# RWKV heads that alternate on the array, and four edits at the end of a two-layer hybrid block

## The chip, the cores and the metric

One core of a Trainium2 chip runs the whole program. The metric is device microseconds of one execution, median of three runs. Five engines work side by side, each through its own queue and in its order: PE (TensorE, matrix products, with its weight loads PEld), DVE (VectorE), ACT (ScalarE), POOL (GpSimd) and SP (SyncE, which issues most DMAs). A matmul of fp32 operands shows as two records of PE in the trace, one of fp32r (the format of the split products) as one.

## The reference, cut to what matters

The block has 256 latent and 256 context tokens of width 1024 and two layers. The change lies in the second layer's RWKV-7 mixer, in its expert sum and in the last norm.

```
# RWKV-7, per head (8 heads of 64), forward and backward over the tokens
def step(s, inp):
    rt, wt, kt, vt, at, bt = inp
    sa = einsum('bhij,bhj->bhi', s, at)
    s = s * wt[:, :, None, :] + sa[..., None] * bt[:, :, None, :] + vt[..., None] * kt[:, :, None, :]
    return s, einsum('bhij,bhj->bhi', s, rt)

# layer 1: S5 and RWKV side by side, then the experts, each with its residual and norm
yl = concatenate([oc_l, od_l], axis=-1)
xl = layer_norm(DEEPNORM_ALPHA * xl + gt1 * (yl @ w_out), ln_g[layer, 0], ln_b[layer, 0])
hl = xl * (1.0 + sc2) + sh2
for e in range(N_EXPERTS):                      # top 2 of 8, gates 0 elsewhere
    out = out + gates[..., e:e + 1] * swiglu(h, wg[e], wu[e], wd[e])
xl = layer_norm(DEEPNORM_ALPHA * xl + gt2 * f, ln_g[layer, 1], ln_b[layer, 1])
```

## The kernel before

The program goes through layer 0 (gated recurrence and attention, dense SwiGLU), the second layer's input products, the stage of S5 and RWKV, the output product with its norm and routing, eight experts, and the last norm. A scheduler fixes the order of each engine's queue when the program is built. Within a queue nothing overtakes: an instruction that waits holds up all behind it.

RWKV's tokens are cut into chunks of 64. The recurrence runs over eight steps `i` in two directions `d` (`SEQ`); steps 0 to 3 are the context, 4 to 7 the latent tokens. Eight heads are held as four pairs `p` of two heads `h`; head h = 0 lies on partitions 0 to 63, h = 1 on 64 to 127. All these products are small, and each uses one part of the array: a product of 64 rows by 64 columns uses a quarter, one of 128 by 64 a half, one of 32 by 32 a sixteenth. Where the two heads follow each other in the code, the parts that they use differ in the columns, the rows or both.

A step (`rwkv_units`, L1834 to L1917) goes: `pq` (state times `lk`, the heads alternate already) -> ACT copies it to `uR` (L1885) -> `pz` (the inverse `uY` times `uR`: four products of head 0, four of head 1) -> copies into `vu`, head 0 by ACT, head 1 by DVE (L1892) -> `ph` (`zh` times `vu`, again head by head) -> DVE adds it to the decayed state `ulT` and writes the new state `uT` (L1907) -> `pq` of the next step. Beside the chain stand `pi`, the 32 by 32 products that complete the inverse for the next step (`unit_inverse`, L1808 to L1828, two rounds with a copy by `evac` between), `gram` and `ztr`, which prepare units two steps ahead (`unit_before`, L1757 to L1806), and the outputs `po` of the latent steps (`outputs`, L1848 to L1862), which run one step late. For each direction and head a `po` bank holds four results; each result is the sum of a product of 128 rows (`uz` times `vu`) and one of 64 rows (`uRr` times `uT`), written in turn. Four products fill 64 rows of the bank, and a copy by ACT or an addition by DVE (L1862) moves them into `rO`.

S5 is put among these steps by generators: `tp<-U,wb` on PE, four multiplications, a sum, a scan and eight `xs` on DVE (L1392 to L1406), then `tp<-ca,xs` on PE. `rwkv_finish` (from L1923) normalises `rO` by heads on DVE and POOL and passes it to the output product.

An expert's last part (`expert`, L2217 to L2237) multiplies the down product by `g`, splits it into `myh` (ACT, L2223) and `myl` (DVE, L2224), and puts the rows back to their tokens by two fp32r products with `back` each; DVE adds the result, weighted, to `x` (L2234). After the eighth expert `norm_out` (L2276 to L2302) does the last norm for two tiles of 128 tokens: statistics, `rstd` (a chain of tiny operations, L205 to L218), and then two operations of DVE per half of 512 columns (L2297, L2298); the first half of tile 0 goes through ACT (L2293) and POOL (L2294, L2295) instead. At the end every engine loads a count of tokens (L2265) and branches on it (L2266).

Of the kernel before, what the change touches and what calls it, by code (L numbers as in the profile page):

```python
# [8 lines left out]
F32 = mybir.dt.float32  # L9
F32R = mybir.dt.float32r  # L10
I32 = mybir.dt.int32
U32 = mybir.dt.uint32
AF = mybir.ActivationFunctionType
OP = mybir.AluOpType
# [151 lines left out]
class Build:  # L166
# [39 lines left out]
    def rstd(self, pool, var, n, eps, op=OP.add):  # L206
# [6 lines left out]
        V.tensor_scalar(y.bitcast(I32), s.bitcast(I32), -1.0, 1597463007.0, op0=OP.mult, op1=OP.add)  # L213
        for _ in range(3):
            V.tensor_mul(w, y, y)
            V.scalar_tensor_tensor(w, w, -0.5, v, op0=OP.mult, op1=OP.mult)
            V.scalar_tensor_tensor(y, w, 1.5, y, op0=OP.add, op1=OP.mult)
# [1539 lines left out]
    def unit_before(self, i, d, rp, lk, zh, zp=None):  # L1757
# [18 lines left out]
        if lat:  # L1776
# [6 lines left out]
            for h in range(2):  # L1783
                pg = p128(f"gram{d}{i}")
                for p in range(4):
                    self.mm(pg[:, p], X[h2(h), p, 0:128], X[h2(h), p, 128:256], True, True)
# [21 lines left out]
    def unit_inverse(self, rp, i, d):  # L1808
# [8 lines left out]
        pb = rp.tile([128, 4, 32], F32, name="uP", tag="uP", bufs=2)  # L1817
        for h in range(2):
            r, o = slice(h * 64 + 32, h * 64 + 64), slice(h * 64, h * 64 + 32)
            for p in range(4):  # L1820
                self.mm(pi[o, 0, p], W[r, p], Y[r, p, 32:64], True, True)
            self.evac(pb[o], pi[o, 0])
        for h in range(2):
            o = slice(h * 64, h * 64 + 32)
            for p in range(4):
                self.mm(pi[o, 1, p], W[o, p], pb[o, p], True, True)
            self.evac(Y[o, :, 32:64], pi[o, 1])
        return Y  # L1828

    def rwkv_units(self, ra, rp, done, inv, room):  # L1830
# [17 lines left out]
        def outputs(i, Ss, vus):  # L1848

            for d in range(2):  # L1850
                n, rows = self.PLACE[self.SEQ[d][i]]
                z, X, S, vu = before[i, d][1], before[i, d][3], Ss[d], vus[d]
                for h in range(2):
                    po = self.psum_mx(f"po{d}{i}")[:, :256].rearrange("p (a b) -> p a b", b=64)
                    for p in range(4):
                        self.mm(po[rows, p], z[:, p, h], vu[:, p, h], True, False)
                        self.mm(po[rows, p], X[h2(h), p], S[h2(h), h, p], False, True)
                    o = O[rows, n].rearrange("p (a h v) -> p a h v", a=4, h=2)[:, :, h]
                    if (d == 0) == (self.SEQ[d][i] < 6):
# [465 lines left out]
```

## Time and profile before

| what | value |
|---|---|
| median of 3 runs | 2151.57 us (2148.89 to 2158.67) |
| the profiled execution, its span | 2162.4 us, 2160.6 us |
| PE busy | 2019.5 us, 93% |
| DVE busy | 1624.6 us, 75% |
| ACT busy | 1048.2 us, 49% |
| POOL busy | 176.3 us, 8% |
| read from and written to HBM | 442.56 MB, 31.98 MB |

The span is the time from the first to the last instruction that the profiler saw. Busy time counts an engine's own work; PE's is modelled at the ends, and the records of pipelined products overlap, so two figures are used for a product: its busy time, and the time from the start of one row to the start of the next. PEclk is the clock that TensorE was granted, as a share of full speed (1.0 is 2.4 GHz, 0.5 is 1.2 GHz); over a stretch it is a mean.

### The profile page before, as it was taken

Reading aid. Unit: us, or ns where it says so; the run is one execution under the profiler, and the core shown is the slowest. Engines: PE = TensorE matmul, PEld = TensorE weight load, DVE = VectorE, ACT = ScalarE, POOL = GpSimd, SP = SyncE. Lnnn points to the kernel's source line nnn. Section 1 sums busy time; section 2 is a strip of 40 time slices with the busy share of each in tenths; the row PEclk is TensorE's granted clock in tenths of the full one; section 3 lists DMA queues with packets and bytes.
Section 4 is the critical chain, followed back from the end, with each engine's and each line's share of the span. In section 5 each row is a group of like instructions: output and inputs, shape, how many; then the busy total and the mean of one; then the engine's idle time right before and its main releaser. Section 6 shows DMA issues by size and latency. Waiting matters only on the chain. (4 is left out here: it accounts for less than half of the span.)

```text
span 2160.6 us, 31186 instructions
## 1 busy us (share of the span) xinstructions
PE 2019.5 (93%) x11518; PEld 1591.5 (74%) x11518; DVE 1624.6 (75%) x3051; ACT 1048.2 (49%) x1604; POOL 176.3 (8%) x222
## 2 busy tenths in 40 slices
PE   7999999999999997895799979999999999999994
PEld 4766777777888876583688857788887777777773
DVE  3566756798777687877554287898989888888886
ACT  3334434332333335651222236777767777677762
POOL 1000000001000011004441033000000000000000
PEclk9999999999999999896666578999999999999997
DMA  8434223347566563477762175999989899998890
GB/s 301 124 109 147 80 78 97 130 151 231 197 195 192 152 169 126 141 226 240 194 177 76 32 267 202 359 344 354 348 328 341 328 346 327 347 331 333 325 357 21
DMA packets 148756, 476.66 MB, mean 221 GB/s; under 512 B 54020, under 2 KB 72532, under 8 KB 113524
## 3 DMA queue, kind: packets, MB, share of 16 engines
q1 hardware_dynamic: 120610, 428.13, 56.4%
q0 software_dynamic: 9648, 34.93, 5.1%
q10 hardware_dynamic: 18338, 11.54, 1.9%
q8 instruction: 92, 1.51, 0.3%
q14 instruction: 68, 0.56, 0.1%
HBM read 442.56 MB, written 31.98 MB: 220 GB/s over the span
## 5 line engine op out<-in xcount | busy, mean ns | idle before, releaser
L201 DVE TENSOR_TENSOR mwl<-mraw,mwh 128x1024 fp32r<-128x1024 f32 x522 | 617.7, 1231 | 57.1 <-ACT mwh L197 52.6
L197 ACT CAST mwh<-mraw 128x1024 fp32r<-128x1024 f32 x528 | 520.3, 1051 | 56.1 <-PE mm L179 32.2
L179 PE MATMUL mm<-hh,wl 128*128 128x512 f32 (+1 forms) x744 | 284.7, 384 | 7.8 <-DVE wl L201 7.8
L179 PE MATMUL mm<-hl,wh 128*128 128x512 f32 (+1 forms) x744 | 286.4, 386 | 4.4 <-DVE hl L452 4.4
L179 PE MATMUL mm<-hh,wh 128*128 128x512 f32 (+1 forms) x744 | 285.9, 387 | 2.7 <-ACT hh L451 2.3
L197 ACT CAST wh<-wraw 128x1024 fp32r<-128x1024 f32 x119 | 124.8, 1050 | 318.3 <-PE mm L179 243.8
L201 DVE TENSOR_TENSOR wl<-wraw,wh 128x1024 fp32r<-128x1024 f32 x119 | 145.1, 1220 | 85.8 <-ACT wh L197 79.5
L179 PE MATMUL mm<-mwh,hgh 128*128 128x512 f32 (+1 forms) x768 | 196.0, 377 | 4.1 <-ACT mwh L197 4.0
L179 PE MATMUL mm<-mwl,hgh 128*128 128x512 f32 (+1 forms) x768 | 196.7, 378 | 2.4 <-DVE mwl L201 2.4
L179 PE MATMUL mm<-mwh,hgl 128*128 128x512 f32 (+1 forms) x768 | 195.7, 377 | 0.0
L179 PEld LDWEIGHTS mm<-hh,wl 128*128 128x128 f32 x744 | 142.9, 192 | 36.7 <-DVE wl L201 9.2
L179 PEld LDWEIGHTS mm<-hh,wh 128*128 128x128 f32 x744 | 141.6, 191 | 34.3 <-ACT wh L197 4.4
L179 PEld LDWEIGHTS mm<-hl,wh 128*128 128x128 f32 x744 | 142.7, 192 | 31.8 <-DVE hl L452 4.8
L179 PEld LDWEIGHTS mm<-mwh,hgh 128*128 128x128 f32 x768 | 136.7, 188 | 34.9 <-ACT mwh L197 5.8
L179 PEld LDWEIGHTS mm<-mwl,hgh 128*128 128x128 f32 x768 | 136.0, 189 | 35.1 <-DVE mwl L201 7.3
L179 PEld LDWEIGHTS mm<-mwh,hgl 128*128 128x128 f32 x768 | 136.6, 188 | 28.6
L179 PE MATMUL mx<-mwh,mah 128*128 128x512 f32 x352 | 103.4, 402 | 1.1 <-ACT mwh L197 1.1
L179 PE MATMUL mx<-mwh,mal 128*128 128x512 f32 x352 | 104.0, 401 | 0.0
L179 PE MATMUL mx<-mwl,mah 128*128 128x512 f32 x352 | 99.8, 399 | 0.0
L179 PEld LDWEIGHTS mx<-mwh,mah 128*128 128x128 f32 x352 | 64.2, 188 | 20.4 <-ACT mwh L197 7.4
L179 PEld LDWEIGHTS mx<-mwl,mah 128*128 128x128 f32 x352 | 65.3, 188 | 14.1
L179 PEld LDWEIGHTS mx<-mwh,mal 128*128 128x128 f32 x352 | 64.7, 188 | 13.4
(600 smaller groups left out, 3283.6 us busy)
## 6 DMA issues: line engine op xcount, KB each, us to landing
mraw<-in_moe_w_dram SPq DMA_DIRECT2D x264, 1024.0 KB, 6.0
adaw<-in_ada_w_dram SPq DMA_DIRECT2D x96, 512.0 KB, 4.9
wraw<-in_ev_w_in_dram SPq DMA_DIRECT2D x26, 512.0 KB, 3.7
wraw<-in_ffn_w_gate_dram SPq DMA_DIRECT2D x22, 512.0 KB, 4.4
wraw<-in_ffn_w_up_dram SPq DMA_DIRECT2D x22, 512.0 KB, 4.4
wraw<-in_ffn_w_down_dram SPq DMA_DIRECT2D x22, 512.0 KB, 4.1
wraw<-in_od_w_in_dram SPq DMA_DIRECT2D x19, 512.0 KB, 4.0
d5ca<-ca POOLq DMA_DIRECT2D x32, 144.0 KB, 4.0
```

The source lines that it names most:

```text
L179: self.nc.tensor.matmul(out, lhsT, rhs, start=start, stop=stop, skip_group_check=True)
L197: self.nc.scalar.copy(hi, raw)
L201: self.nc.vector.tensor_sub(lo, raw, hi.bitcast(F32))
```

## The change

It has five parts. In `gram` of the latent chunks, `pi`, `pz` and `ph` the loop over heads goes inside the loop over pairs, so that the products of the two heads alternate; the copies follow when both heads are done, and the latent `gram` uses its two banks at once. In `outputs` both directions write one bank per head, into different row groups; first come all products of 128 rows, then all of 64 rows, with the directions in turn, and one copy or addition of 128 partitions replaces two of 64. The last expert's `back` and `my` stay fp32 and are multiplied without a split. The last norm is done by DVE alone, `rstd` of a single column has two operations fewer, and the output leaves in halves, those of tile 1 on two queues. The statement that loads the count stands in `moe_route`'s `later`.

```diff
@@ -211,9 +211,14 @@
         V.tensor_scalar(v, var, eps, None, op0=op)
         V.tensor_scalar(s.bitcast(I32), v.bitcast(I32), 1, None, op0=OP.logical_shift_right)
         V.tensor_scalar(y.bitcast(I32), s.bitcast(I32), -1.0, 1597463007.0, op0=OP.mult, op1=OP.add)
+        if n == 1:
+            V.tensor_scalar(v, v, -0.5, None, op0=OP.mult)
         for _ in range(3):
-            V.tensor_mul(w, y, y)
-            V.scalar_tensor_tensor(w, w, -0.5, v, op0=OP.mult, op1=OP.mult)
+            if n == 1:
+                V.tensor_scalar(w, y, y, v, op0=OP.mult, op1=OP.mult)
+            else:
+                V.tensor_mul(w, y, y)
+                V.scalar_tensor_tensor(w, w, -0.5, v, op0=OP.mult, op1=OP.mult)
             V.scalar_tensor_tensor(y, w, 1.5, y, op0=OP.add, op1=OP.mult)
         return y
 
@@ -1780,10 +1785,11 @@
             nc.gpsimd.tensor_mul(R, X[:, :, 192:256], r)
             nc.gpsimd.tensor_copy(X[:, :, 192:256], R)
             z = zp.tile([128, 4, 2, 64], F32, name="uz", tag="uz", bufs=6)
-            for h in range(2):
-                pg = p128(f"gram{d}{i}")
-                for p in range(4):
-                    self.mm(pg[:, p], X[h2(h), p, 0:128], X[h2(h), p, 128:256], True, True)
+            pgs = [p128(f"gram{d}{i}") for _ in range(2)]
+            for p in range(4):
+                for h in range(2):
+                    self.mm(pgs[h][:, p], X[h2(h), p, 0:128], X[h2(h), p, 128:256], True, True)
+            for h, pg in enumerate(pgs):
                 V.tensor_mul(lk[h2(1 - h), h], pg[hi, :, 0:64], bc(tri[hi, 0]))
                 V.tensor_mul(z[:, :, h], pg[:, :, 64:128], bc(tri[:, 1 + d]))
         else:
@@ -1815,16 +1821,18 @@
         nc.scalar.dma_start(Y, self.d_y[d, ch].rearrange("i p t -> p i t"))
         pi = self.psum_mx(f"pi{d}{i}")[:, :256].rearrange("p (n a b) -> p n a b", n=2, a=4)
         pb = rp.tile([128, 4, 32], F32, name="uP", tag="uP", bufs=2)
+
+        r, o = ([slice(h * 64 + s, h * 64 + s + 32) for h in range(2)] for s in (32, 0))
+        for p in range(4):
+            for h in range(2):
+                self.mm(pi[o[h], 0, p], W[r[h], p], Y[r[h], p, 32:64], True, True)
         for h in range(2):
-            r, o = slice(h * 64 + 32, h * 64 + 64), slice(h * 64, h * 64 + 32)
-            for p in range(4):
-                self.mm(pi[o, 0, p], W[r, p], Y[r, p, 32:64], True, True)
-            self.evac(pb[o], pi[o, 0])
+            self.evac(pb[o[h]], pi[o[h], 0])
+        for p in range(4):
+            for h in range(2):
+                self.mm(pi[o[h], 1, p], W[o[h], p], pb[o[h], p], True, True)
         for h in range(2):
-            o = slice(h * 64, h * 64 + 32)
-            for p in range(4):
-                self.mm(pi[o, 1, p], W[o, p], pb[o, p], True, True)
-            self.evac(Y[o, :, 32:64], pi[o, 1])
+            self.evac(Y[o[h], :, 32:64], pi[o[h], 1])
         return Y
 
     def rwkv_units(self, ra, rp, done, inv, room):
@@ -1847,19 +1855,22 @@
 
         def outputs(i, Ss, vus):
 
-            for d in range(2):
-                n, rows = self.PLACE[self.SEQ[d][i]]
-                z, X, S, vu = before[i, d][1], before[i, d][3], Ss[d], vus[d]
-                for h in range(2):
-                    po = self.psum_mx(f"po{d}{i}")[:, :256].rearrange("p (a b) -> p a b", b=64)
-                    for p in range(4):
-                        self.mm(po[rows, p], z[:, p, h], vu[:, p, h], True, False)
-                        self.mm(po[rows, p], X[h2(h), p], S[h2(h), h, p], False, True)
-                    o = O[rows, n].rearrange("p (a h v) -> p a h v", a=4, h=2)[:, :, h]
-                    if (d == 0) == (self.SEQ[d][i] < 6):
-                        nc.scalar.copy(o, po[rows])
-                    else:
-                        V.tensor_add(o, o, po[rows])
+            po = [self.psum_mx(f"po{i}{h}")[:, :256].rearrange("p (a v) -> p a v", a=4) for h in range(2)]
+            where = [self.PLACE[self.SEQ[d][i]] for d in range(2)]
+            n = where[0][0]
+            assert where[1][0] == n
+
+            for k in range(2):
+                for p, h in heads:
+                    for d, (_, rows) in enumerate(where):
+                        l, r = ((before[i, d][1][:, p, h], vus[d][:, p, h]), (before[i, d][3][h2(h), p], Ss[d][h2(h), h, p]))[k]
+                        self.mm(po[h][rows, p], l, r, k == 0 and p == 0, k == 1)
+            for h in range(2):
+                o = O[:, n].rearrange("p (a h v) -> p a h v", a=4, h=2)[:, :, h]
+                if i < 6:
+                    nc.scalar.copy(o, po[h])
+                else:
+                    V.tensor_add(o, o, po[h])
 
         left = None
         for i in range(8):
@@ -1886,9 +1897,9 @@
                 Rs.append(R)
             for d in range(2):
                 pz = p64(f"pz{d}{i}")
+                for p, h in heads:
+                    self.mm(pz[h2(h), p], inv[i, d][h2(h), p], Rs[d][h2(h), p], True, True)
                 for h in range(2):
-                    for p in range(4):
-                        self.mm(pz[h2(h), p], inv[i, d][h2(h), p], Rs[d][h2(h), p], True, True)
                     (V.tensor_copy if h else nc.scalar.copy)(vus[d][lo, :, h], pz[h2(h)])
             if not last:
                 for d in range(2):
@@ -1900,9 +1911,9 @@
                         t = rp.tile([128, 4, 64], F32, name="ulT", tag="ulT", bufs=2)
                         for h in range(2):
                             nc.gpsimd.tensor_mul(t[h2(h)], S[h2(h), h], dec[h2(h), :, None].to_broadcast([64, 4, 64]))
+                    for p, h in heads:
+                        self.mm(ph[h2(h), p], zh[:, p, h2(h)], vus[d][:, p, h], True, True)
                     for h in range(2):
-                        for p in range(4):
-                            self.mm(ph[h2(h), p], zh[:, p, h2(h)], vus[d][:, p, h], True, True)
                         if i:
                             V.tensor_add(N[h2(h), h], t[h2(h)], ph[h2(h)])
                         else:
@@ -2069,6 +2080,8 @@
             V.tensor_reduce(cf[:, 1, 0:1], cf[:, 0], axis=AX.X, op=OP.max)
             V.tensor_copy(self.count[:, 0], cf[:, 0])
             V.tensor_copy(self.count[:, 1, 0:1], cf[:, 1, 0:1])
+            self.most = nc.values_load(self.count[0:1, 1, 0:1], min_val=0, max_val=256,
+                                       skip_runtime_bounds_check_because="a count of 256 tokens")
 
         return later
 
...
@@ -2218,8 +2231,11 @@
 
             for h in range(2):
                 y = mp.tile([128, 512], F32, name="my", tag="ma", bufs=2)
+                V.tensor_mul(y, dn[h], self.g2[:, h * 512:h * 512 + 512])
+                if exact:
+                    ys.append((y,))
+                    continue
                 yh, yl = (mp.tile([128, 512], F32R, name=f"my{n_}", tag=f"ma{n_}", bufs=3) for n_ in "hl")
-                V.tensor_mul(y, dn[h], self.g2[:, h * 512:h * 512 + 512])
                 nc.scalar.copy(yh, y)
                 V.tensor_sub(yl, y, yh.bitcast(F32))
                 ys.append((yh, yl))
@@ -2228,8 +2244,8 @@
             for t in range(2):
                 for h in range(2):
                     ps = self.psum_tp()
-                    for n_ in range(2):
-                        self.mm(ps, back[:, t * 128:t * 128 + 128], ys[h][n_], n_ == 0, n_ == 1)
+                    for n_, y in enumerate(ys[h]):
+                        self.mm(ps, back[:, t * 128:t * 128 + 128], y, n_ == 0, n_ == len(ys[h]) - 1)
                     o = self.x[1][:, t, h * 512:h * 512 + 512]
                     V.scalar_tensor_tensor(o, ps, self.gate[:, t, e:e + 1], o, op0=OP.mult, op1=OP.add)
                 if then is not None:
@@ -2253,17 +2269,16 @@
             if e + 1 < NE:
                 def gather(e=e):
                     nonlocal nxt
-                    nxt = self.expert_gather(e + 1, 0)
+                    nxt = self.expert_gather(e + 1, 0, e + 2 == NE)
                 todo[3] = gather
-            scale, put = self.expert(e, *cur, ahead if e == 0 else (), todo, scale)
+            scale, put = self.expert(e, *cur, ahead if e == 0 else (), todo, scale, e + 1 == NE)
         gb = self.norm_factors(3)
         room = lambda: self.mx.tile([128, 2, D], F32, name="o", tag="mraw", bufs=1)
         o = room()
         scale()
         put(lambda t: self.norm_out(t, gb, o))
 
-        most = nc.values_load(self.count[0:1, 1, 0:1], min_val=0, max_val=256, skip_runtime_bounds_check_because="a count of 256 tokens")
-        with tc.If(most > 128):
+        with tc.If(self.most > 128):
             for e in range(NE):
                 n = nc.values_load(self.count[0:1, 0, e:e + 1], min_val=0, max_val=256, skip_runtime_bounds_check_because="a count of 256 tokens")
                 with tc.If(n > 128):
@@ -2284,21 +2299,17 @@
             V.bn_stats(st[:, h], x[:, h * 512:h * 512 + 512])
         V.bn_aggr(mv, st)
         rs = self.rstd(self.lnp, mv[:, 1:2], 1, 1e-5)
-        if t == 0:
-            nb = self.lnp.tile([128, 1], F32, name="nb2")
-            V.scalar_tensor_tensor(nb, mv[:, 0:1], -1.0, rs, op0=OP.mult, op1=OP.mult)
+        to = self.a["out"].rearrange("(a b) d -> a b d", b=64)
         for h in range(2):
             hs = slice(h * 512, h * 512 + 512)
-            if t == 0 and h == 0:
-                nc.scalar.activation(o[:, hs], x[:, hs], AF.Identity, bias=nb, scale=rs)
-                nc.gpsimd.tensor_mul(o[:, hs], o[:, hs], g[:, hs])
-                nc.gpsimd.tensor_add(o[:, hs], o[:, hs], b[:, hs])
+            V.scalar_tensor_tensor(o[:, hs], x[:, hs], mv[:, 0:1], g[:, hs], op0=OP.subtract, op1=OP.mult)
+            V.scalar_tensor_tensor(o[:, hs], o[:, hs], rs, b[:, hs], op0=OP.mult, op1=OP.add)
+            if t == 0:
+                nc.sync.dma_start(self.a["out"][64:192, hs], o[:, hs])
             else:
-                V.scalar_tensor_tensor(o[:, hs], x[:, hs], mv[:, 0:1], g[:, hs], op0=OP.subtract, op1=OP.mult)
-                V.scalar_tensor_tensor(o[:, hs], o[:, hs], rs, b[:, hs], op0=OP.mult, op1=OP.add)
-            to = self.a["out"][:, hs]
-            to = to.rearrange("(a b) d -> a b d", b=64)[::3] if t else to[64:192]
-            (nc.sync if h else nc.scalar).dma_start(to, o[:, hs])
+
+                nc.sync.dma_start(to[0, :, hs], o[0:64, hs])
+                nc.scalar.dma_start(to[3, :, hs], o[64:128, hs])
 
 
 _INPUTS = ['x', 'c', 'ctx', 'c_ctx', 'ada_w', 'ada_b', 'ln_g', 'ln_b', 'ev_w_in', 'ev_w_out', 'hg_lb', 'hg_norm_g',
```

The first place is PE's queue in step 2 of the recurrence, behind the `pq` products of both directions; `pz` and `ph` come in one tile for each direction, `pi` is the inverse for step 3, `gram` a unit two steps ahead, `tp<-ca` is S5's readout.

```order
 L179 MATMUL pq_10241<-uT,lk 64x64 x8
-L179 MATMUL pz_10252<-uR,uY 64x64 x4
-L179 MATMUL pz_10263<-uR,uY 64x64 x4
-L179 MATMUL pz_10252<-uR,uY 64x64 x4
-L179 MATMUL ph_10274<-vu,zh 64x64 x4
-L179 MATMUL pz_10263<-uR,uY 64x64 x4
-L179 MATMUL pi_10308<-uY,uW 32x32 x4
-L179 MATMUL pi_10334<-uY,uW 32x32 x4
...
+L179 MATMUL pz_10252<-uR,uY 64x64 x8
+L179 MATMUL pz_10263<-uR,uY 64x64 x8
+L179 MATMUL ph_10274<-vu,zh 64x64
+L179 MATMUL pi_10308<-uY,uW 32x32 x8
+L179 MATMUL pi_10334<-uY,uW 32x32 x8
+L179 MATMUL gram_10366<-uX 128x128 x4
+L179 MATMUL tp<-U,wb_10422 64x64
+L179 MATMUL tp<-ca_10147,xs 32x128 x4
...
+L179 MATMUL ph_10274<-vu,zh 64x64 x7
```

Blocks of four products of one head have become blocks of eight in which the heads alternate. Of `ph`, one product stands alone ahead of `pi`, and the other seven stand behind S5's readout.

The second place is PE's queue where the outputs of step 4 are formed, before the change; `po14` is the bank of direction 1 for one head, `po04` that of direction 0 for the next.

```order
L179 MATMUL po14_11162<-vu_10724,uz_10123 64x64
L179 MATMUL po14_11162<-uT_10578,uRr_10120 64x64
L179 MATMUL po14_11162<-vu_10724,uz_10123 64x64
L179 MATMUL po14_11162<-uT_10578,uRr_10120 64x64
L179 MATMUL po04_11152<-vu_10720,uz_10091 64x64
L179 MATMUL po04_11152<-uT_10563,uRr_10088 64x64
```

The same place after the change; `po41` is the bank of head 1 in step 4, `vu_10720` and `uT_10563` are of direction 0, `vu_10724` and `uT_10578` of direction 1.

```order
L179 MATMUL po41_11143<-vu_10720,uz_10091 64x64
L179 MATMUL po41_11143<-vu_10724,uz_10123 64x64
L179 MATMUL po41_11143<-vu_10720,uz_10091 64x64
L179 MATMUL po41_11143<-vu_10724,uz_10123 64x64
L179 MATMUL po41_11143<-uT_10563,uRr_10088 64x64
L179 MATMUL po41_11143<-uT_10578,uRr_10120 64x64
```

The products of 128 rows and of 64 rows no longer alternate one by one; within each kind the two directions do.

The third place is the end of SP's queue, before the change, from the last expert load to the branch.

```order
L2143 DMA mraw_19285<-in_moe_w_dram 128x2048
L2143 DMA mraw_19307<-in_moe_w_dram 128x2048
L2301 DMA out_0_dram<-o_19331 128x512
L2301 DMA out_0_dram<-o_19331 2x64x512
L2265 TENSOR_LOAD count_11717
L2266 COMPARE_AND_BRANCH
```

The same place after the change.

```order
L2156 DMA mraw_19272<-in_moe_w_dram 128x2048
L2156 DMA mraw_19294<-in_moe_w_dram 128x2048
L2308 DMA out_0_dram<-o_19318 128x512 x2
L2311 DMA out_0_dram<-o_19318 64x512 x2
L2083 TENSOR_LOAD count_11701
L2281 COMPARE_AND_BRANCH
```

The load of the count has another line number and stands where it stood, directly ahead of the branch; it does so on the other four engines too. Outside the stage of S5 and RWKV and the program's end, the queues hold the same instructions in the same order, but for a few neighbours that change places among the experts.

## Rows read from the trace of the kernel before

**Rows 1.** Windows of the whole program: start:end, length, busy (instructions), PEclk, DMA share, GB/s.
```profile
1027.00:1257.70 230.70, 217.53 (x2209) 177.15 (x2206) 113.42 (x315) 49.96 (x145) 61.58 (x88) 0.65 0.47 123
...
1345.00:2129.00 784.00, 775.56 (x3610) 624.45 (x3610) 692.98 (x692) 558.02 (x641) 0.00 (x0) 1.00 0.88 331
```

**Rows 2.** Windows from one step's first pq to another's: PE, PEld, DVE, ACT, POOL.
```profile
1036.98:1151.46 114.48, 111.12 (x1357) 92.69 (x1353) 66.68 (x175) 26.09 (x82) 45.48 (x64) 0.66 0.62 159
1151.46:1192.46 41.00, 41.00 (x388) 33.73 (x384) 19.48 (x55) 9.49 (x28) 9.29 (x15) 0.69 0.28 72
1192.46:1230.32 37.86, 37.86 (x269) 29.88 (x268) 8.50 (x24) 6.35 (x20) 1.09 (x2) 0.55 0.07 19
1230.32:1257.70 27.38, 26.36 (x186) 20.18 (x186) 15.01 (x48) 7.21 (x13) 3.89 (x6) 0.72 0.46 137
```

**Rows 3.** The same windows, tile po on PE alone.
```profile
1151.46:1192.46 41.00, 12.99 (x66) 0.69 0.28 72
1192.46:1230.32 37.86, 20.00 (x100) 0.55 0.07 19
1230.32:1257.70 27.38, 13.33 (x90) 0.72 0.46 137
```

**Rows 4.** The same windows, tile pz on PE: steps 0 to 4, and the sum.
```profile
1036.98:1151.46 114.48, 14.55 (x160) 0.66 0.62 159
...
sum 220.72, PE 22.40; mean PE 5.60
```

**Rows 5.** The same windows, tile ph on PE: steps 0 to 4, and the sum.
```profile
1036.98:1151.46 114.48, 17.38 (x160) 0.66 0.62 159
...
sum 220.72, PE 24.87; mean PE 6.22
```

**Rows 6.** The same windows, tile pi on PE: steps 0 to 4, and the sum.
```profile
1036.98:1151.46 114.48, 23.17 (x352) 0.66 0.62 159
...
sum 220.72, PE 33.35; mean PE 8.34
```

**Rows 7.** Timeline of PE, blocks at granted clock 0.50: start, us, what, records.
```profile
1056.66 0.69 PE L179 MATMUL gram<-uX 64*64 64x64 f32 x8
...
1136.09 1.12 PE L179 MATMUL pq<-uT,lk 128*64 128x64 f32 x16
1137.14 1.11 PE L179 MATMUL pz<-uR,uY 64*64 64x64 f32 x8
...
1140.22 1.11 PE L179 MATMUL ph<-vu,rt 128*64 128x64 f32 x8
1141.26 1.06 PE L179 MATMUL pi<-uY,uW 32*32 32x32 f32 x16
```

**Rows 8.** Timeline of PE, first and last of 24 po rows (clock 0.50), of 14 (1.00).
```profile
1210.24 0.48 PE L179 MATMUL po<-vu,uz 128*64 128x64 f32 x2
...
1219.52 0.47 PE L179 MATMUL po<-uT,uRr 64*64 64x64 f32 x2
...
1238.76 0.33 PE L179 MATMUL po<-vu,uz 128*64 128x64 f32 x2
...
1242.09 0.47 PE L179 MATMUL po<-uT,uRr 64*64 64x64 f32 x2
```

**Rows 9.** Timeline of DVE in step 2: the last xs and the last new state.
```profile
1104.96 0.22 DVE L1406 TENSOR_TENSOR xs<-rt,rt 64x64 f32<-64x64 f32 x1
...
1109.86 0.42 DVE L1907 TENSOR_TENSOR uT<-ulT,ph 64x256 f32<-64x256 f32 x1 [0.36 <-PE ph L179]
```

**Rows 10.** Timeline of DVE at the program's end.
```profile
2130.04 1.29 DVE L2224 TENSOR_TENSOR myl<-my,myh 128x512 fp32r<-128x512 f32 x2
...
2140.48 0.75 DVE L2298 SCALAR_TENSOR_TENSOR o<-o,nwt,gb 128x512 f32<-128x512 f32 x1
...
2143.00 2.30 DVE L2298 SCALAR_TENSOR_TENSOR o<-o,nwt,gb 128x512 f32<-128x512 f32 x2
```

**Rows 11.** Timeline of POOL at the program's end.
```profile
2142.83 1.26 POOL L2295 TENSOR_TENSOR o<-o,gb 128x512 f32<-128x512 f32 x1
```

## Prediction of the time

> **What bounds the kernel now.** I read the windows of the whole program first. Between 1345 and 2129 us, in the experts, PE is busy 775.56 of 784.00 us at full clock, and the change touches nothing there but the last expert's end. In the stage of S5 and RWKV PE is busy 217.53 of 230.70 us, at a mean clock of 0.65, while DVE works 113.42 us and ACT 49.96 us [rows 1]. So this stage too is PE's, though its products are tiny, and that is where the loops change.
>
> The second view cuts the stage at the first `pq` of steps. In steps 5 and 6 PE has no gap at all, 41.00 of 41.00 and 37.86 of 37.86 us, with DVE at 19.48 and 8.50 us. Steps 0 to 4 have 111.12 of 114.48 us, but DVE works 66.68 us there [rows 2]. The reader is to see two kinds of step: in 5 and 6 nothing but PE sets the length, in 0 to 4 DVE stands not far behind.
>
> The third view takes one tile at a time. `po` holds PE for 12.99, 20.00 and 13.33 us in steps 5, 6 and 7, together 46.3 us [rows 3], `pz` 22.40 [rows 4], `ph` 24.87 [rows 5], `pi` 33.35 us [rows 6].
>
> The fourth is PE's timeline, for prices by the order of the products. All blocks of rows 7 ran at clock 0.50, and two records are one product. `pq`, whose heads alternate already, does eight products in 1.12 us. `ph`, of the same shape, does four of one head in 1.11 us, and `pz` four in 1.11. `gram` of a context chunk, 64 by 64 like `pz` but with alternating heads, does four in 0.69 us [rows 7]. So alternating costs between a half and 0.62 of one head after the other. `po` is worst: its 24 rows between 1210.24 and 1219.52 are 23 starts in 9.28 us, 0.40 us for one product, with the two shapes in turn and a change of shape at each; at clock 1.00 the 14 rows from 1238.76 to 1242.09 give 0.26 us [rows 8]. Against `pq`'s 1.12 / 8 = 0.14 us that is almost three times as much.
>
> **The change part by part.** *Outputs.* The same 128 products remain. Instead of a change of shape at each of them there are four blocks in a step, in which two column groups alternate. If a product then costs what it costs in `pq`, the ratio is 0.14 / 0.40 = 0.35, and 46.3 us become 16.2: 30.1 us of PE freed, 8.4 in step 5, 13.0 in step 6, 8.7 in step 7. The other bound is the price of `gram`, 0.69 / 4 = 0.17 us, ratio 0.43: 26.4 us. I take 30, as most blocks are longer than `gram`'s four. Sixteen copies and additions of 64 partitions become eight of 128; this is off PE's path and counts nothing in steps 5 and 6, where DVE and ACT have room [rows 2].
>
> *pz.* Between 0.50 (as `pq` to `ph`) and 0.62 (as `gram`), I take 0.55: 22.40 x 0.45 = 10.1 us, of which 14.55 x 0.45 = 6.5 in steps 0 to 4 [rows 4].
>
> *ph.* The order shows that the first product goes alone and seven follow later, so I take 0.60: 24.87 x 0.40 = 9.9 us, 17.38 x 0.40 = 7.0 of it in steps 0 to 4 [rows 5].
>
> *pi.* No row has 32 by 32 products whose heads alternate. Eight of them with one change of head took 1.06 us [rows 7]. The bounds are no gain, and a half, 16.7 us. I take 0.58, between the two ratios above, since the two heads lie in different rows and columns as `gram`'s do: 33.35 x 0.42 = 14.0 us, 23.17 x 0.42 = 9.7 in steps 0 to 4 [rows 6]. The latent `gram` alternates too; its moving side is 128 columns long, and I allow it 2 us, half of it in steps 0 to 4.
>
> Freed on PE: 30.1 + 10.1 + 9.9 + 14.0 + 2.0 = 66 us. Steps 0 to 4 hold 6.5 + 7.0 + 9.7 + 1.0 = 24; step 7 holds `po`'s 8.7 and an eighth of `pz`'s 10.1, some 10; steps 5 and 6 the remaining 32.
>
> *What is given back.* In steps 0 to 4 DVE is late next. In step 2 its last `xs` starts at 1104.96 us, and behind it in the queue stand the copy to `vu` and the additions, the last at 1109.86 [rows 9]; `pq` of step 3 can't start before, however fast PE gets there. DVE's 66.68 of 114.48 us [rows 2] leave room on the mean, but in short steps like this one there is nearly none. I count two thirds, 16 of 24. In step 5 DVE has 19.48 of 41.00 us, S5's last generator in its first part, so I count 11.5 of 14.6. Step 6 has no such work, and all of its 17.4 counts. Step 7 ends in `rwkv_finish`, a chain through DVE and POOL whose products for the second half of the tokens come last; PE's saving there shortens only what stands ahead of the last `rO`, and I count 2.5 of 10. Sum: 16 + 11.5 + 17.4 + 2.5 = 47.4 us. DMA does not give it back: its share is 0.07 in step 6 [rows 2], and SP's first loads for the experts stand behind this stage in the program, so they move forward with it.
>
> *The last expert's rows.* `myl` on DVE goes, 1.29 us for two [rows 10], and ACT's cast ahead of the put products; each pair of fp32r products becomes one fp32 product of two records. The trace has no fp32 product of 512 columns. Taken as two records like the two that go, nothing is lost; taken as twice that, four products lose some 2 us, of which one or two lie on the path. I take a gain of 0.7.
>
> *The last norm.* Two operations of DVE of 512 columns are added, 2 x 0.75 = 1.5 us by the one that stands free. But POOL's two go, and while they run DVE is slow: the two L2298 beside POOL's L2295 [rows 11] took 2.30 us, 0.8 more than two of 0.75 [rows 10]. POOL's other operation meets DVE just before, and I allow it another 0.8, by the same rows. Five tiny operations go as well; counted at 0.2 us each, an estimate a little above what a row's share of the chain would be, they give 1.0. Sum 0.8 + 0.8 + 1.0 - 1.5 = 1.1 us gained, between a loss of 0.5 (if those operations were slow for another reason) and a gain of 2. The output in more and smaller pieces changes what follows the last operation by less than half a microsecond either way, I estimate.
>
> *The count.* The order shows the load directly ahead of the branch as before, with nothing between. It counts 0.
>
> **The sum.** 47.4 + 0.7 + 1.1 = 49.2 us. The profiled execution took 2162.4 us, so 2113.2 by its own time. The runs' median of 2151.57 lies 10.8 us below it; I take that off unchanged: 2102.4, forecast 2102 us.
>
> The Trainium skill speaks against a part of it. Its page TensorEngine Tiling (Array Packing), section Restrictions and Gotchas, says that different row tiles cannot access the same PSUM bank simultaneously. The alternating `pz`, `pi` and `ph` results of both heads go to one bank; `ph` uses all rows, so the rule would bear on `pz` and `pi`. In the trace `gram` of a context chunk alternates row tiles within one bank, and took 0.69 us for four products where `pz` took 1.11 [rows 7], which the rule would not let it do. By the rule the result is rival C.
>
> **The rivals.**
> *A, the clock falls.* The mean of 0.65 [rows 1] is 30% of the time at 2.4 GHz and 70% at 1.2. Less work on PE may leave all of the stage at 1.2 GHz. Then the part at full clock, 0.3 x (217.5 - 66) = 45 us, takes 0.40 / 0.26 times as long [rows 8], 24 us more, of which a third falls into gaps that are there anyway: gain 49 - 16 = 33, so 2119 us. For it: step 6 ran at 0.55 while PE was never idle [rows 2]. Against: step 7 had gaps and ran at 0.72 [rows 2], so idle time alone did not bring the low level.
>
> *B, the clock rises.* If alternating heads bring the stage to 2.4 GHz, the 70% at half clock, 0.7 x 151 = 106 us, shrink by (0.40 - 0.26) / 0.40 [rows 8]: 37 us, half of it lost to DVE. Gain 67, 2085 us. For it: the experts, with PE busy 775.56 of 784.00 us, are at 1.00 [rows 1]. Against: step 6 with no gap at all was not [rows 2].
>
> *C, two heads don't overlap in one bank.* Then `pz` and `pi` keep their time; `po`, which has a bank for each head, and `ph` free 40 us, 7.0 in steps 0 to 4, 9.7 in step 5, 14.7 in step 6 and 8.7 in step 7. Passed on in the proportions above: 4.7 + 7.5 + 14.7 + 2.5 = 29, with the end 31: 2121 us. Against it stands `gram`'s 0.69 us [rows 7].
>
> *D, slower: `ph` behind DVE.* PE's queue now holds seven `ph` products that need DVE's copy of head 1, which stands behind the eight `xs`; before, only four of eight stood there. While they wait nothing behind them on PE runs. The price today, from the last `xs` to the last state, is 5 us in step 2 [rows 9]. To eat the gain, the wait must grow by 49 / 7 = 7 us in each of the seven steps with `ph`, and beyond 60 / 7 = 8.6 us the kernel is slower by over 0.5%: at 10 us in each, 70 - 49 = 21 us more, 2173 us. PE's freed time makes such waits visible, but DVE's own work does not grow, so I give it little.
>
> **How the numbers follow.** The forecast, 2092 to 2113 us by the bounds of `po`, `pi` and of the two thirds, 0.50; A 0.17, B 0.15, C 0.12, D 0.02. The remaining 0.04 is a stage where DVE sets nearly every step and less than 11 us come through. Together A to C and the forecast fill 2080 to 2124 us, which is the range; some 0.15 to 0.2 lie outside. A difference under 0.5%, 10.8 us, can't be told from none: faster by more, 0.93; within, 0.05; slower, 0.02.
>
> **What would show it.** In the profile after: `po` near 16 us in all, `pz` near 12, `ph` 15, `pi` 19; the stage near 183 us instead of 230.7, with gaps on PE ahead of `ph`, `pq` and `tp<-ca` in steps 0 to 4, put down to DVE, and hardly any in step 6; DVE's L2298 at 0.7 us each. I am wrong if `pz` and `pi` keep their time, if PE's gaps grow as much as its busy time falls, or if the stage's clock moves to either level.

## The result and the profile after

The changed kernel took 2075.05 us (median of 4 runs, 2073.38 to 2084.47), the one before 2155.12 us in its 4: ratio 0.9642, 95% interval 0.9604 to 0.968, 80 us faster. The forecast was 2102 us. The profiled executions differ by 77.9 us, with spans of 2160.6 and 2082.7 us, so they can be set side by side:

| stretch | before | after | difference | forecast |
|---|---|---|---|---|
| steps 0 to 4 | 114.5 | 100.2 | -14.3 | -16 |
| step 5 | 41.0 | 23.1 | -17.9 | -11.5 |
| step 6 | 37.9 | 11.5 | -26.4 | -17.4 |
| step 7, to the last `po` | 27.4 | 18.7 | -8.7 | -2.5 |
| last `po` to the last down product | 871.4 | 871.3 | -0.1 | 0 |
| from there to DVE's last operation | 16.2 | 14.9 | -1.3 | -1.8 |
| from there to the end of the span | 15.3 | 6.7 | -8.6 | 0 |

The windows of the changed kernel, cut at the same products as [rows 2]; the columns are PE, PEld, DVE, ACT, POOL, PEclk, DMA share and GB/s.

```profile
1036.41:1136.60 100.19, 87.34 (x1389) 70.70 (x1385) 67.54 (x180) 26.41 (x84) 45.92 (x66) 0.74 0.73 185
1136.60:1159.74 23.14, 21.19 (x368) 17.72 (x365) 17.13 (x48) 7.68 (x22) 8.11 (x12) 1.00 0.47 124
1159.74:1171.24 11.50, 10.94 (x239) 9.73 (x238) 8.02 (x21) 5.37 (x17) 1.56 (x2) 1.00 0.23 60
1171.24:1189.93 18.69, 15.00 (x202) 11.90 (x201) 15.69 (x59) 6.75 (x14) 3.92 (x6) 0.75 0.59 173
```

Two things stand in it. In steps 5 and 6 the granted clock went from 0.69 and 0.55 to 1.00. It shows in products that no edit touches: the `mm` of step 6, products of S5's rows with `gw`, have 25 records in both kernels and took 6.97 us before and 3.64 after.

```profile
1192.46:1230.32 37.86, 6.97 (x25) 0.55 0.07 19
```

```profile
1159.74:1171.24 11.50, 3.64 (x25) 1.00 0.23 60
```

And in steps 0 to 4 PE now has gaps, 12.9 us, with DVE busy 67.5 of 100.2 us.

The sums by tile on PE, in the order `po`, `pz`, `ph`, `pi` ([rows 3 to 6] of before):

```profile
sum 153.45, PE 11.66; mean PE 2.92
...
sum 153.45, PE 11.49; mean PE 2.87
...
sum 153.45, PE 14.40; mean PE 3.60
...
sum 153.45, PE 16.45; mean PE 4.11
```

Forecast were 16.2, 12.3, 15 and 19.3 us. What PE waits for longest in the stage now (engine, tile, line, releaser: us, times, longest):

```profile
PE tp L179 <- DVE xs L1411: 6.8, 5, 3.5
PE gram L179 <- POOL uX L1786: 2.3, 2, 1.4
PE pq L179 <- DVE z L1401: 2.3, 1, 2.3
```

PE's timeline gives the prices of blocks after the change, at clock 0.50 (1126 and 1188 us) and 1.00 (1174 and 1175):

```profile
1126.38 1.12 PE L179 MATMUL pz<-uR,uY 64*64 64x64 f32 x16
...
1174.08 1.15 PE L179 MATMUL pz<-uR,uY 64*64 64x64 f32 x32
...
1175.54 0.69 PE L179 MATMUL po<-uT,uRr 64*64 64x64 f32 x32
...
1188.81 1.12 PE L179 MATMUL po<-uT,uRr 64*64 64x64 f32 x16
```

At half clock eight `pz` cost 1.12 us, where four did before [rows 7]; at full clock sixteen cost as much. An output product of 64 rows costs 0.04 us at full clock where both heads and directions take turns (sixteen in 0.69 us), and 0.14 at half clock with the two directions of one head (eight in 1.12), in place of 0.26 and 0.40 [rows 8].

The end, from DVE's last operation on, first before, then after; only the DMA share and GB/s, the last two columns, are of interest.

```profile
2145.30:2160.60 15.30, 0.00 (x0) 0.00 (x0) 0.00 (x1) 0.00 (x0) 0.00 (x0) 0.50 0.14 47
```

```profile
2076.04:2082.70 6.66, 0.00 (x0) 0.00 (x0) 0.00 (x0) 0.00 (x0) 0.00 (x0) 0.50 0.29 86
```

Before, the last output goes out at 47 GB/s with 0.14 of 16 DMA engines busy, about two of them.

### The profile page after: what moved, and what is told of

Same layout as the page of the kernel before. It is cut to its first block, busy times and chain, and to the rows that moved or that the text cites. A ratio compares the mean times of both kernels' runs of the same rounds, so it can differ in the third digit from the quotient of the medians.

```text
span 2082.7 us, 31141 instructions
## 1 busy us (share of the span) xinstructions
PE 1937.9 (93%) x11518; PEld 1524.4 (73%) x11518; DVE 1621.9 (78%) x3038; ACT 1044.0 (50%) x1597; POOL 172.4 (8%) x220
## 4 chain that ended last, share of the span: by engine, by line
PE 80%; DVE 9%; DMA 5%; issue 2%; ACT 2%; POOL 1%; SPq 0%; DVEq 0%; ACTq 0%; POOLq 0%
PE mm L179 50%; PE mx L179 14%; PE ax L179 7%; PE tp L179 3%; PE tp L183 3%; DVE mwl L201 2%; DMA adaw<-in_ada_w_dram 2%; PE ztr L179 1%; POOL udl L1806 1%; PE gram L179 1%; DMA uX<-drx 1%; DVE wl L201 1%; DMA dt<-in_s_ldt_dram 1%; PE pi L179 0%; DMA ca<-d5ca 0%
## 5 line engine op out<-in xcount | busy, mean ns | idle before, releaser
L201 DVE TENSOR_TENSOR mwl<-mraw,mwh 128x1024 fp32r<-128x1024 f32 x522 | 618.1, 1233 | 56.8 <-ACT mwh L197 53.4
```

The costliest lines, as they stand in the source:

```text
L201: self.nc.vector.tensor_sub(lo, raw, hi.bitcast(F32))
```

## The experiments

Each kernel ran beside runs of the kernel before on the same chip. The lead-in to the stage, some 1030 us that no edit touches, differs by up to 17 us between the profiled executions of these kernels, more than some of the effects, so lengths of stretches are compared, and whole times only where the interval carries it. Stretches scatter too: steps 0 to 4 in the old order took between 110.4 and 115.3 us in four traces (the kernel before and the versions with the output split, the shapes in order and the directions in turn). Steps 5 and 6 in the old order have two traces. That of the version with the output split, whose edit lies behind them, repeats the 41.0 and 37.9 us and the clocks of the kernel before:

```profile
1149.19:1190.19 41.00, 41.00 (x388) 33.72 (x385) 19.50 (x55) 9.50 (x28) 9.31 (x15) 0.69 0.26 72
1190.19:1228.04 37.85, 37.85 (x269) 29.89 (x268) 8.49 (x24) 6.36 (x20) 1.09 (x2) 0.55 0.07 19
```

Beside these versions the kernel before took 2131 to 2163 us in 27 executions, with a mean clock of 0.948 over the shortest and 0.929 over the longest. So the clock moves in it without an edit too: in the two traces of the old order just named it was 0.66 and 0.69 in steps 0 to 4; the shorter executions have no trace.

**The outputs alone.**

```diff
-            for d in range(2):
...
-                for h in range(2):
-                    po = self.psum_mx(f"po{d}{i}") ...
...
+            po = [self.psum_mx(f"po{i}{h}") ... for h in range(2)]
...
+            for k in range(2):
+                for p, h in heads:
+                    for d, (_, rows) in enumerate(where):
...
```

> The kernel before with the new order of the output products alone (one bank per head, both directions in it, 128-row products first, 64-row products after). Theory 'order': po falls from 46.3 us of PE to 16 or less at whatever clock is granted, and steps 5 to 7 keep their clocks of 0.69, 0.55, 0.72: 25 to 28 us faster. Theory 'clock': with the changes of shape gone the chip grants PEclk 1.00 in steps 5 and 6, and all that is left there shrinks too: 38 to 42 us faster. Steps 0 to 4 keep 114 us in both. The end, from the last operation of DVE on, stays 15 us.

2114.95 us, ratio 0.9836 (0.9778 to 0.9893). `po` fell to 13.6 us; the stage from 220.7 to 177.7.

```profile
1034.70:1145.40 110.70, 107.38 (x1356) 89.71 (x1352) 67.14 (x175) 26.09 (x82) 45.33 (x64) 0.69 0.64 163
1145.40:1176.90 31.50, 31.31 (x388) 26.92 (x384) 19.09 (x55) 8.37 (x25) 8.90 (x15) 0.81 0.35 93
1176.90:1194.70 17.80, 17.80 (x255) 15.61 (x254) 6.79 (x19) 5.22 (x16) 1.49 (x2) 0.86 0.14 39
1194.70:1212.40 17.70, 14.13 (x203) 11.46 (x202) 14.94 (x58) 6.75 (x14) 3.92 (x6) 0.90 0.54 153
```

Steps 5 to 7 give 39 us, as 'clock' said, though the clock rose to 0.81 to 0.90 and not to 1.00; the whole time fell by 35 us, with an interval that covers both theories. The 110.7 us of steps 0 to 4 lie within the scatter of the old order.

**The alternating heads alone**, in `gram`, `pi`, `pz` and `ph` (their four hunks of the diff ahead).

```diff
-                for h in range(2):
-                    for p in range(4):
-                        self.mm(pz[h2(h), p], ...)
+                for p, h in heads:
+                    self.mm(pz[h2(h), p], ...)
```

> The kernel before with the heads alternating in pz, ph, pi and the latent gram, and the outputs as before. Both theories: steps 0 to 4 go from 114 to about 100 us, as in the changed kernel, where DVE's S5 chain sets them. Theory 'order': steps 5 and 6 give another 4 each, 20 to 24 us in all, and their PEclk stays at 0.55 to 0.7, since the output products fill them. Theory 'clock' in the form that any alternation brings full clock: 1.00 in step 6 and 30 us or more. If the rule on row tiles in one bank held, pz and pi would keep 22 and 33 us and the gain would be under 8 us.

2116.0 us, ratio 0.9853 (0.9797 to 0.9909). Stage 184.1 us, 36.6 less. Steps 0 to 4 take 101.0 us, as expected; `pz` and `pi` fall to 11.3 and 16.5 us, so the bank rule doesn't hold for their time here.

```profile
1122.90:1155.00 32.10, 31.37 (x368) 25.63 (x365) 18.87 (x52) 8.55 (x24) 9.29 (x15) 0.79 0.34 93
1155.00:1180.90 25.90, 25.79 (x259) 20.45 (x258) 9.20 (x25) 6.57 (x21) 1.38 (x2) 0.76 0.10 27
```

The clock of steps 5 and 6 rose here too, to 0.79 and 0.76, with the old outputs in them, so 'order' was wrong on the clock and, by the stage, on the gain, and 'clock' on its 1.00. The two halves add up to 80 us where both together give 67.

**One order of shapes, nothing alternating.**

```diff
-                    for p in range(4):
-                        self.mm(po[rows, p], z[:, p, h], vu[:, p, h], True, False)
-                        self.mm(po[rows, p], X[h2(h), p], S[h2(h), h, p], False, True)
+                    for p in range(4):
+                        self.mm(po[rows, p], z[:, p, h], vu[:, p, h], p == 0, False)
+                    for p in range(4):
+                        self.mm(po[rows, p], X[h2(h), p], S[h2(h), h, p], False, True)
```

> The kernel before with the output products of one bank put in the order of their shape: four of 128 rows, then four of 64, nothing alternates. Theory 'shape': most of po's price is the change of shape at each product; blocks of four cost what pz's blocks of four did, 1.05 us at half clock and some 0.65 at full, so po falls from 46 us to 20 to 33, by the clock. Theory 'neighbours' (most is won by the two directions in different column groups): po stays above 38 us.

One run, 2121.98 us. `po` takes 22.2 us, the stage 187.4. Up to step 5 it runs as the kernel before did [rows 2]; from there the same products in another order of shapes ran at 0.99 and 1.00:

```profile
1034.80:1150.10 115.30, 112.27 (x1356) 93.58 (x1353) 67.17 (x176) 26.09 (x82) 46.42 (x65) 0.65 0.62 158
1150.10:1179.60 29.50, 28.90 (x390) 24.67 (x386) 18.71 (x52) 9.19 (x27) 8.33 (x13) 0.99 0.39 100
1179.60:1199.30 19.70, 19.70 (x269) 17.20 (x268) 8.30 (x23) 5.84 (x18) 1.56 (x2) 1.00 0.14 36
```

The view of `po` alone, from step 5 on:

```profile
1148.00:1222.20 74.20, 22.16 (x256) 0.94 0.37 104
```

**The directions in turn, the shape changed after every two products** (the kernel before with the new outputs, the two loops swapped in them).

```diff
-            for k in range(2):
-                for p, h in heads:
+            for p, h in heads:
+                for k in range(2):
```

> The kernel before with one output bank per head and the two directions in turn, but the shape changes after every two products. Theory 'shape': the 64 changes that are left cost nearly as much as each product did before, 0.26 us at full clock and 0.40 at half, so po takes 20 to 28 us, well above the 13.6 of the version grouped by shape and direction. Theory 'neighbours': po near 14 us, as there.

One run, 2129.59 us; `po` takes 22.5 us, PEclk is 0.89, 0.77 and 0.70 in steps 5 to 7, the stage takes 190.0 us.

```profile
1148.00:1225.50 77.50, 22.45 (x256) 0.80 0.33 96
```

So the order of shapes alone, or the directions in turn with half of the changes left, brings `po` from 46 to 22 us; the directions in turn and four blocks in a step bring it to 13.6. The clock carries a part of each: from step 5 on its mean was 0.94 and 0.80 here and 0.85 with the outputs alone, against 0.55 to 0.72 before. Both expectations by 'shape' hold.

**Alternating only from step 4 on** (in `pz` and `ph` by `if lat`, in `pi` for units from 5).

```diff
+        if i < 5:
+            for h in range(2):
...
+                for p in range(4):
+                    self.mm(pi[o, 0, p], W[r, p], Y[r, p, 32:64], True, True)
...
```

> The changed kernel, but in pz, ph of steps 0 to 3 and in pi of units 1 to 4 the heads follow each other as before. Steps 0 to 4 take some 108 to 111 us, as with the outputs alone. Theory 'own order': the clock of steps 5 and 6 is set by the order inside them; PEclk 1.00 and steps 5 to 7 at 53 us, as in the changed kernel. Theory 'what ran ahead': the clock there depends on what the array did before; PEclk 0.8 to 0.9 as with the outputs alone, and 58 to 64 us.

One run, 2071.34 us. Steps 0 to 3, step 4, and steps 5 to 7:

```profile
1027.10:1110.10 83.00, 80.14 (x1073) 67.13 (x1071) 55.06 (x139) 21.21 (x67) 40.69 (x55) 0.76 0.75 197
1110.10:1123.90 13.80, 13.71 (x321) 11.23 (x317) 11.63 (x37) 5.17 (x18) 5.12 (x10) 1.00 0.59 141
1123.90:1177.29 53.39, 46.49 (x807) 38.63 (x803) 41.96 (x130) 19.71 (x53) 14.77 (x22) 0.94 0.47 133
```

Steps 5 to 7 took 53.4 us, as 'own order' said. But steps 0 to 3 took 83.0 us without alternation in `pz`, `ph` and `pi`, and 82.8 with it, and step 4 13.8 in place of 17.4: the expected 108 to 111 us for steps 0 to 4 was wrong, it was 96.8.

**`gram` and outputs**, the two edits together on the kernel before.

> The kernel before with two edits: the new outputs, and the latent gram with alternating heads in two banks. Between the outputs alone (steps 0 to 4: 110.7 us) and the version with late alternation (96.8) lie gram, step 4's pz and ph, and pi from unit 5 on. Theory 'gram': its two banks are filled side by side and DVE gets both at once, so most of the 14 us is won here: 97 to 101 us. Theory 'clock': steps 3 and 4 go from 0.77 and 0.53 to 1.00 only with step 4's own alternation: 107 to 111 us, and step 4 at 0.5 to 0.6.

One run, 2109.62 us; steps 0 to 4 took 101.4 us, just above what 'gram' said, and step 4 ran at 0.82, where 'clock' said 0.5 to 0.6. So `gram`'s two banks and alternating heads are enough for most of what steps 0 to 4 gain. Whether `pz`, `ph` and `pi` without them would be enough as well, no run shows. The view of `gram` over steps 0 to 4, with the outputs alone and here:

```profile
1034.70:1145.40 110.70, 16.10 (x104) 0.69 0.64 163
```

```profile
1038.80:1140.20 101.40, 14.38 (x104) 0.78 0.70 182
```

Their PEclk is 0.78 where the outputs alone had 0.69; `gram`'s own time there fell only from 16.1 to 14.4 us, so the rest came by the clock and by what DVE gets earlier, which these runs do not part.

**The output split.**

```diff
-            to = to.rearrange("(a b) d -> a b d", b=64)[::3] if t else to[64:192]
-            (nc.sync if h else nc.scalar).dma_start(to, o[:, hs])
+            q = nc.sync if h else nc.scalar
+            if t:
+                to = to.rearrange("(a b) d -> a b d", b=64)
+                q.dma_start(to[0], o[0:64, hs])
+                q.dma_start(to[3], o[64:128, hs])
...
```

> The kernel before with one edit: each output DMA of tile 1 (2x64x512) becomes two of 64x512 on the same queue. Theory 'spread': the 2x64x512 transfer runs on two DMA engines only (its DMA share is 0.13, 2 of 16), and two of 64 rows use all: 7.5 to 9.5 us less from DVE's last operation to the end, 8.6 faster in all. Rival 'end of program': those 15.2 us are the engines' barrier, the load of the count and the branch, and become shorter in the changed kernel for another reason: less than 1 us.

2140.13 us, ratio 0.9949 (0.9916 to 0.9982). From DVE's last operation to the end 7.6 us in place of 15.3:

```profile
2143.02:2150.60 7.58, 0.00 (x0) 0.00 (x0) 0.00 (x1) 0.00 (x0) 0.00 (x0) 0.50 0.35 95
```

**The changed kernel without that split.**

```diff
-                nc.sync.dma_start(to[0, :, hs], o[0:64, hs])
-                nc.scalar.dma_start(to[3, :, hs], o[64:128, hs])
+                (nc.sync if h else nc.scalar).dma_start(to[::3, :, hs], o[:, hs])
```

> The changed kernel with tile 1's output put back into one DMA of 2x64x512 for each half, on SP and ACT as before. Theory 'spread': 8.6 us of the gain is lost (7.5 to 9.5), so about 71 us faster than the kernel before instead of 80, and DVE's last operation to the end is 15 us again instead of 6.7. Rival 'end of program': under 1 us lost, 79 to 80 faster.

2089.67 us, ratio 0.9717 (0.9664 to 0.977); the end takes 15.2 us again. 'Spread' holds both ways for the end; the whole time lies 60 us under the kernel before, at the edge of the interval from the 71 expected.

**Both copies into `vu` on ACT**, in the changed kernel.

```diff
-                    (V.tensor_copy if h else nc.scalar.copy)(vus[d][lo, :, h], pz[h2(h)])
+                    nc.scalar.copy(vus[d][lo, :, h], pz[h2(h)])
```

> The changed kernel with the copy of head 1 into vu on ACT instead of DVE. Theory 'DVE floor': in steps 0 to 4 ph waits behind S5's eight xs in DVE's queue; without that copy ph runs ahead of the readout and steps 0 to 4 shrink from 100 us to 94 to 98: 82 to 86 us faster than the kernel before in place of 80. Rival: the additions that write the new state stay behind the xs on DVE, so the next pq starts no earlier: within 1 us of the changed kernel in that stage, or slower where ACT's copies queue behind its S5 outputs.

2073.14 us, ratio 0.9649 (0.9581 to 0.9717): the stage takes 149.6 us and steps 0 to 4 take 96.7, as 'DVE floor' said, against 98.8 to 100.2 in three traces that differ from it in nothing ahead of the last norm but this copy. In the whole time there is no difference that can be told.

The changed kernel again, beside the next two.

> The changed kernel itself, timed beside the next two. Both theories: its stage of S5 and RWKV takes 153 to 154 us again and the kernel is 75 to 80 us faster than the one before.

2071.61 us, ratio 0.9628 (0.9583 to 0.9674), the stage takes 152.3 us, at PEclk 0.73, 1.00, 1.00 and 0.74 over the four stretches, as in the first trace. Step 6 ran at 1.00 in all seven traces that have the new outputs and alternate from step 4 on. Step 5 did in six; in the changed kernel without the output split, with the same products in this stage, it had 0.86 and took 25.1 us:

```profile
1135.75:1160.82 25.07, 24.10 (x369) 20.36 (x365) 18.00 (x50) 7.71 (x22) 9.21 (x14) 0.86 0.44 120
```

Late alternation again, timed.

> Heads alternate only from step 4 on, timed. Theory 'early alternation brings nothing' (steps 0 to 3 took 83.0 us without it and 82.8 with it): the stage takes 150 us again, PEclk 1.00 from step 3 to step 6, and the time lies 0 to 5 us under the changed kernel's. Rival 'the clock of that one look was luck': the stage differs by more than 3 us from 150.2, and steps 0 to 4 come out near the 111 us that the outputs alone left.

2078.41 us, ratio 0.9665 (0.9619 to 0.971). The profiled stage took 152.5 us, no less than the changed kernel's 152.3 beside it: steps 0 to 3 took 86.9 us against 81.5 there, step 4 13.8 against 17.5. Expected was a time 0 to 5 us under the changed kernel's; it lies 6.8 us above, with intervals that overlap. Early alternation brings the stage nothing that can be told, and leaving it out wins nothing either.

Late alternation with both copies on ACT.

> The same with both copies into vu on ACT. Theory 'DVE floor': steps 0 to 4 lose another 2 to 4 us, as they did in the changed kernel (153.5 to 149.6), stage 146 to 148. Rival: without early alternation PE hardly waits for DVE (1.1 us), so the copy's engine doesn't matter: 150 us, within 1 us.

2102.34 us, ratio 0.9775 (0.9729 to 0.9821): slower than either edit alone by over 20 us, against both expectations. The stage took 170.2 us, 17.7 more than with late alternation alone. Steps 0 to 3 and step 4, first of this version, then of that with late alternation alone, timed beside it:

```profile
1036.95:1137.65 100.70, 95.87 (x1156) 79.13 (x1153) 53.91 (x140) 25.79 (x80) 43.25 (x61) 0.69 0.64 170
1137.65:1154.00 16.35, 16.35 (x229) 12.88 (x226) 8.46 (x28) 3.89 (x14) 3.03 (x5) 0.51 0.25 66
```

```profile
1024.50:1111.40 86.90, 84.33 (x1074) 70.89 (x1071) 54.79 (x139) 21.22 (x67) 39.76 (x55) 0.71 0.71 187
1111.40:1125.20 13.80, 13.59 (x321) 11.16 (x318) 11.65 (x37) 5.25 (x18) 5.14 (x10) 1.00 0.65 142
```

Steps 0 to 3 lost 13.8 us at nearly the same mean clock; the cause is open. In step 4 PE never paused and stayed at half clock, where the other had 1.00. No version tried beats the changed kernel by more than the runs scatter.

## Why the prediction was wrong

**Right.** That PE sets the stage; that alternating products cost about half, within one bank too, so rival C fell; the last expert's rows and the norm (1.3 of 1.8 us; by DVE's timeline 0.75 where 0.7 was forecast, and 0.6 where 1.1 was); the count, since the end takes 15.2 us with the load moved and the output unsplit, and 15.3 before; and D didn't come: PE has no wait of `ph` for DVE in the stage. The 6.8 us behind the `xs` are those of S5's readout `tp<-ca`, which stands ahead of the seven `ph`.

**Wrong: "46.3 us become 16.2", and its like.** These ratios were prices at half clock, put on times that held the old mix of clocks; a rise of the clock was left to rival B, whose 2085 us came nearest. Taken at the old clock, the terms of steps 5 and 6 hold in sum, by an estimate from the windows above. Sixteen records of `pz` cost 1.12 us at half clock and 1.15 / 2 at full, a factor of about 1.9. Step 6 has 10.94 us of PE at full clock; at 0.55, a tenth of the time at full, that would be 10.94 / (0.1 + 0.9 / 1.9) = 19.1 us, with its 0.6 us of gaps 18.2 less than before, where 17.4 was forecast. The remaining 8.2 us of its 26.4 are the clock. In step 5, at 0.69, 21.19 us become 21.19 / (0.38 + 0.62 / 1.9) = 30.0, with its 2 us of gaps 9 less than before (11.5 forecast), and 8.8 of its 17.9 are the clock. So about 17 of the 31 us by which the gain was undersized are the clock's. The order of products in these steps goes with it: 0.55 in step 6 in both traces of the old order, 1.00 in all seven of the new. The version with the shapes in order and nothing else points the same way, in one trace: the same stage up to there, then 0.99 and 1.00. Why a level is granted stays open: step 5 of the new order had 0.86 once, the clock rose in part with the old outputs (0.76 in step 6), and in one version two edits that each did no harm left step 4 at 0.51.

**Wrong: "changes what follows the last operation by less than half a microsecond".** It was 8.6 us, shown in both directions. The row was there to be read: after the last operation of DVE the trace of before has 15.3 us in which only the output moves, at a DMA share of 0.14. A transfer whose outer dimension is 2 went to about 2 of the 16 DMA engines (0.14 x 16 = 2.2). The Trainium skill says so: in DMA: Bandwidth & Descriptors, Rules for kernel authors, an outermost dimension smaller than 16 confines a DMA to at most that many engines. The trace agrees, and the prediction did not use it.

**Wrong: step 7, "I count 2.5 of 10".** It gave 8.7. The prediction let PE's saving shorten only what stands ahead of the last `rO` and counted little for that. `rwkv_finish` for the first half of the tokens starts when step 6's outputs are added, and before the change these additions waited for PE. The last addition of them, before (released by `po`) and after (x2 is both heads), on DVE's timeline:

```profile
1240.40 0.41 DVE L1862 TENSOR_TENSOR rO<-rO,po 64x256 f32<-64x256 f32 x1 [0.93 <-PE po L179]
```

```profile
1176.48 0.76 DVE L1873 TENSOR_TENSOR rO<-rO,po 128x256 f32<-128x256 f32 x2
```

It ends 10.5 us after the step's beginning before (1230.32) and 6.0 after (1171.24): 4.5 us, a part of it again by the clock, 0.77 and 1.00 up to there. From this addition to PE's products that turn the result (`mx<-ident,rO`, at 1251.49 and 1186.77) there are 10.7 and 9.5 us, 1.2 less. Behind them stands the second half of step 7's own `po`, where the prediction let PE's saving shorten nothing: 6.2 and 3.2 us to the last one, 3.0 less.

**Right by luck.** Steps 0 to 4 came out near the forecast, 14.3 us less where 16 were forecast, but 23.2 of the 24.2 us that it put in for PE there were `pz`, `ph` and `pi`, and only 1.0 `gram`; `gram` and the new outputs without the other three brought them to 101.4 us. Without alternation in `pz`, `ph` and `pi` of steps 0 to 3, and with `gram` alternating, steps 0 to 4 took 96.8 and 100.7 us in two traces, against 98.8 to 100.2 with it.

## What to carry to other kernels

Price small products by their neighbours: an output product cost 0.40 us between products of another shape and 0.14 between products of its own shape on other columns, both at half clock. When such an edit fills or thins a stage, work out its time at both levels of TensorE's clock and give the two a real chance each, since the level moved with the order here. And read the last stretch of a program, where no engine is busy, by its DMA share: here a share of 0.14 was output on about two of the 16 DMA engines, and splitting it gave 7.7 us.

## What was not expected of the hardware

PE can be busy without a pause and be granted 1.2 GHz for nearly all of the time: step 6 of before, 37.86 of 37.86 us at a mean of 0.55, and 16.35 us at 0.51 in the last experiment; and it kept 2.4 GHz through steps 5 and 6 after the change, with 8% and 5% of gaps. Two edits that each left the stage within 4 us of the changed kernel's 152.3 lengthened it together by 18 us (152.5 to 170.2, one trace, and by over 20 us in the times of four runs), and why is open.
